# Low halves of streamed weights: from a VectorE subtraction to a ScalarE negation and an accumulating DMA

## Chip, cores and metric

The kernel runs on one core of a Trainium2 chip. The metric is the device time of one execution in microseconds (us). An execution is also recorded by the hardware profiler; its trace gives the start and duration of every instruction and DMA packet. Engines are named as in the profile: PE is TensorE, with PEld for its weight loads, DVE is VectorE, ACT is ScalarE, POOL is GpSimd, SP is SyncE. SP does no arithmetic here; it issues DMAs.

## The reference, cut to what matters

A two-layer trunk on 16 meta tokens and 512 frames of width 1024, in float32. Layer 0 mixes by two kinds of attention, layer 1 by retention in chunks; each layer ends with a squared-ReLU MLP of width 4096, and a layer norm stands behind each half.

```python
for layer in range(DEPTH):                       # DEPTH = 2
    i = layer // 2
    if layer % 2 == 0:
        mix = _even_mixer(h, even_w_in[i], ..., even_w_out[i], layer)
    else:
        mix = _retention(h, ret_w_in[i], ret_w_out[i])
    h = _layer_norm(DEEPNORM_ALPHA * h + mix, ln_g[layer, 0], ln_b[layer, 0])
    h = _layer_norm(DEEPNORM_ALPHA * h + _sq_relu_mlp(h, ffn_w1[layer], ffn_w2[layer]),
                    ln_g[layer, 1], ln_b[layer, 1])
```

All matrices together are 224 tiles of 128 x 1024 floats (512 KB), each used once.

## The kernel before

**Two halves.** A float32 product is made of three passes of a faster format, fp32r. Every operand is split into a high half, the value rounded to fp32r, and a low half, the value minus the high half. A product is high x high + high x low + low x high (`PASSES`, issued in `product`), so for each block of a weight the third matmul is the first that reads the weight's low half. On the chip's page the halves of weights are `wh` and `wl`.

**How a weight comes.** `weight_plan` lists the tiles in the order of use. `prepare` (line 211) takes the next: it takes one of three raw buffers (`rpool`), has SP load the tile from HBM into it (line 223), and calls `halves` (line 226). There ScalarE casts the raw tile to `wh` (line 228), and VectorE subtracts, `wl` = raw - `wh` (line 229). The raw buffer is free for a later load when both have read it. `weights` (line 264) is called by each product for its tile, and first prepares tiles until two ahead of it exist. The halves live in `upool`, 43 buffers that all other large tiles share.

**Quads.** For three quarters of each MLP's first matrix the kernel computes a 2 x 2 block product from seven block products instead of eight. `quad_steps` (line 232) prepares such a quad from two raw tiles, r0 and r1, in five steps: the halves of r0 ("11" and "22"), sums of blocks of r0 and r1 (lines 242, 248, 250) with their own halves ("a" to "d"), and the halves of one half of r1, named `w12` in the code (lines 252 and 253). `quad_up` (line 1138) multiplies; its results go through the banks qa to qd, and ScalarE and VectorE turn them into `tv`, `up` and `g`. There are 24 quads.

**Other stages.** A stage that ends in a layer norm is written by `tail`, which runs its last six tiles over the first half of the positions and then over the second, so that the norm of one half runs beside products of the other. `begin` starts the next MLP with the first half that is ready.

**What sets the order.** A scheduler orders each engine's instructions when the program is built; an engine then runs its own list strictly in order and waits at semaphores. A wait of ScalarE for a product, say, also holds a cast that stands behind it. SP's list holds DMAs alone. GpSimd has no work but four small memsets at the start.

The subtraction that the diff replaces is line 229 when it is called for a raw tile, and line 253. The halves of sums (line 229 on `sums`) stay as they are, and so do the first four tiles, which are loaded by `load` (line 369) instead of SP's plain call.

Of the kernel before, what the change touches and what calls it, by code (L numbers as in the profile page):

```python
# [9 lines left out]
F32R = mybir.dt.float32r  # L10
AF = mybir.ActivationFunctionType
ALU = mybir.AluOpType
# [100 lines left out]
def plan_tiles(plan):  # L113
    first, n = [], 0
    for item in plan:
        first.append(n)
        n += 2 if item[0] == "Q" else 1
    return first
# [3 lines left out]
def kernel(  # L122
# [19 lines left out]
    nc = tc.nc  # L142
    act, dve = nc.scalar, nc.vector
# [18 lines left out]
    first_tile = plan_tiles(plan)  # L162
# [8 lines left out]
    def both(dt=F32, name="u"):  # L171
        return upool.tile([P, 2, L], dt, tag="u", name=name)
# [5 lines left out]
    def flat(dt, name):  # L178
        return both(dt, name).rearrange("p a b -> p (a b)")[:, :1024]

    def raw_tile():
        return rpool.tile([P, 1024], F32, tag="raw", name="raw")
# [10 lines left out]
    def f(t):  # L193
        return t.bitcast(F32)

    def dup(t, n):
        return t.rearrange("p (o n) -> p o n", o=1).broadcast_to([P, 2, n])
# [8 lines left out]
    queue = {"next": 0, "used": 0, "ready": []}  # L206
# [4 lines left out]
    def prepare(load=nc.sync.dma_start):  # L211
        i = queue["next"]
        if i == len(plan):
            return
        queue["next"] += 1
        if plan[i][0] == "Q":
            quad = {}
            quad["steps"] = quad_steps(quad, first_tile[i])
            next(quad["steps"])
            queue["ready"].append(quad)  # L220
            return
        raw = raw_tile()
        load(out=raw, in_=w[first_tile[i]])
        queue["ready"].append(halves(raw))

    def halves(raw):
        wh, wl = flat(F32R, "wh"), flat(F32R, "wl")
        act.copy(out=wh, in_=raw)  # L228
        dve.tensor_tensor(out=wl, in0=raw, in1=f(wh), op=ALU.subtract)  # L229
        return wh, wl  # L230

    def quad_steps(quad, at):
        lo, hi = slice(0, 512), slice(512, 1024)
        r0, r1 = raw_tile(), raw_tile()
        nc.sync.dma_start(out=r0, in_=w[at])
        nc.sync.dma_start(out=r1, in_=w[at + 1])
        yield
        h, l = halves(r0)
        quad["11"], quad["22"] = (h[:, lo], l[:, lo]), (h[:, hi], l[:, hi])
        yield  # L240
        s0 = flat(F32, "sums")
        dve.tensor_tensor(out=s0.rearrange("p (a b) -> p a b", a=2), in0=r0.rearrange("p (a b) -> p a b", a=2),  # L242
                          in1=dup(r1[:, hi], 512), op=ALU.add)
        yield
        h, l = halves(s0)
        quad["c"], quad["a"] = (h[:, lo], l[:, lo]), (h[:, hi], l[:, hi])
        s1 = flat(F32, "sums")
        dve.tensor_tensor(out=s1[:, lo], in0=s0[:, hi], in1=r0[:, lo], op=ALU.add)
        yield
        dve.tensor_tensor(out=s1[:, hi], in0=s1[:, lo], in1=r1[:, lo], op=ALU.add)  # L250
        t = flat(F32R, "w12")
        act.copy(out=t[:, lo], in_=r1[:, lo])
        dve.tensor_tensor(out=t[:, hi], in0=r1[:, lo], in1=f(t)[:, lo], op=ALU.subtract)
        quad["12"] = t[:, lo], t[:, hi]
        yield
        h, l = halves(s1)
        quad["b"], quad["d"] = (h[:, lo], l[:, lo]), (h[:, hi], l[:, hi])
# [6 lines left out]
    def weights(kind, ahead=2):  # L264
        while queue["next"] < min(len(plan), queue["used"] + 1 + (1 if kind == "Q" else ahead)):
            prepare()
        assert plan[queue["used"]][0] == kind
        queue["used"] += 1
        if kind == "Q":
            quad = queue["ready"].pop(0)  # L270
            for _ in quad["steps"]:
                pass
            return quad
        wh, wl = queue["ready"].pop(0)
        k, n = {"A": (8, P), "B": (2, 512), "C": (4, 256)}[kind]
        return tuple(t.rearrange("p (k n) -> p k n", k=k, n=n) for t in (wh, wl))
# [92 lines left out]
    def load(out, in_):  # L369
        dma = nc.sync.dma_start(out=out, in_=in_)  # L370
        if loads["last"] is not None:
            after(dma, loads["last"])
        loads["last"] = dma
        return dma

    prepare(load)
    for j in range(KT // 2):
        raw = both(F32, "xf")
        for i in range(2):
            load(raw[:, i, :], x[2 * j + i])  # L380
        for i in range(2):
            pair = both(F32R, "s")
            xs.append(split(raw[:, i, :], dst=(pair[:, 0, :], pair[:, 1, :])))
            act.copy(out=hm[:, 2 * j + i, :4 * META].rearrange("p (a c n) -> p a c n", a=2, c=2),
                     in_=f(pair)[:, :, :META].rearrange("p a (o n) -> p a o n", o=1).broadcast_to([P, 2, 2, META]))
        if j < 3:
            prepare(load)
# [459 lines left out]
    for h in range(8):  # L847
# [5 lines left out]
        else:  # L853
            if h == 6:
                for j in range(KT // 2):
                    t = both(F32, "y")
# [378 lines left out]
    for k, (ps, outs, pairs) in enumerate(early):  # L1235
        for i in (6, 7):
# [5 lines left out]
                lambda span, t=ht: layer_norm(span, 0, t))  # L1242
# [236 lines left out]
```

## Time and profile before

| | us |
|---|---|
| three runs: lowest, median, highest | 1528.26, 1532.27, 1533.14 |
| the profiled execution, its own time | 1526.21 |
| its span in the profile | 1524.4 |
| TensorE busy | 1485.1 |
| VectorE busy | 922.8 |
| ScalarE busy | 609.4 |

The span is the time from the first instruction to the last in the trace. The granted clock of TensorE was 0.994 on average. The page's second part cuts the span into 40 slices and shows tenths of busy time in each:

```profile
PE   8999999999999999999999999999999999999997
...
DVE  4574466677758576568534354254477848676567
ACT  4474444536324233245343442153445524233323
...
DMA  6111102141313323243014035022150313313221
```

TensorE has hardly a slice under 9, and the transfers come in bursts. In a row of groups, the text after the engine is operation, what is written <- what is read, and the shapes; then the count, the busy total, the mean of one in ns, and the idle time ahead of them with what ended it.

### The profile page before, as it was taken

The page shows a single profiled execution, that of the slowest core. Times are in us where ns is not written, and L with a number is a line of the kernel's source. Part 1 is how long each engine was busy: PE and PEld are TensorE (multiplying, and loading weights), DVE is VectorE, ACT ScalarE, POOL GpSimd, SP SyncE. Part 2 cuts the span into 40 slices and gives each one's busy share as a digit, 9 for nine tenths or more (in the row PEclk, how much of TensorE's full clock was granted, in tenths as well). Part 3 has the DMA queues.
Part 4 walks back from the last instruction along what each step waited for, and adds up shares of the span by engine and source line. Part 5 has one row for each costly group of instructions (what it writes and reads, how often), then busy time and mean ns, then how long its engine had stood idle before and what let it go on. Part 6 is the DMA issues. An engine that isn't in the chain of part 4 may idle for free.

```text
span 1524.4 us, 23188 instructions
## 1 busy us (share of the span) xinstructions
PE 1485.1 (97%) x9752; PEld 1334.4 (88%) x9752; DVE 922.8 (61%) x1522; ACT 609.4 (40%) x972; POOL 0.2 (0%) x4
## 2 busy tenths in 40 slices
PE   8999999999999999999999999999999999999997
PEld 6887878799999999999888888888899888898986
DVE  4574466677758576568534354254477848676567
ACT  4474444536324233245343442153445524233323
POOL 0000000000000000000000000000000000000000
PEclk9999999999999999999999999999999999999999
DMA  6111102141313323243014035022150313313221
GB/s 243 51 48 55 56 29 85 57 138 32 97 55 91 116 70 125 71 132 117 28 42 137 14 109 166 0 89 90 56 168 27 111 56 97 124 62 133 83 70 56
DMA packets 39593, 129.02 MB, mean 85 GB/s; under 512 B 4725, under 2 KB 7173, under 8 KB 39489
## 3 DMA queue, kind: packets, MB, share of 16 engines
q1 hardware_dynamic: 39488, 127.54, 26.1%
q8 instruction: 76, 1.25, 0.3%
q14 instruction: 29, 0.23, 0.0%
HBM read 125.43 MB, written 2.10 MB: 84 GB/s over the span
## 4 chain that ended last, share of the span: by engine, by line
PE 86%; DVE 9%; ACT 2%; DMA 2%; issue 1%; ACTq 0%; DVEq 0%
PE bank L156 33%; PE mm L156 21%; PE v_ps L156 10%; PE qc L156 5%; PE o_ps L156 5%; PE s_ps L156 4%; DVE wl L229 3%; PE qa L156 3%; DMA raw<-in_w 2%; PE qd L156 2%; ACT wh L228 1%; PE t_ps L159 1%; PE qb L156 1%; PE sum_ps L156 1%; DVE up L1182 1%
## 5 line engine op out<-in xcount | busy, mean ns | idle before, releaser
L229 DVE TENSOR_TENSOR wl<-raw,wh 128x1024 fp32r<-128x1024 f32 x200 | 242.3, 1221 | 71.6 <-ACT wh L228 70.9
L228 ACT CAST wh<-raw 128x1024 fp32r<-128x1024 f32 x200 | 205.9, 1046 | 107.7 <-DMA raw<-in_w 75.8
L156 PE MATMUL bank<-g,wh 128*128 128x512 f32 (+2 forms) x800 | 202.3, 344 | 3.4 <-ACT g L1183 2.9
L156 PEld LDWEIGHTS bank<-g,wh 128*128 128x128 f32 x800 | 138.4, 190 | 22.0 <-ACT g L1183 3.1
L156 PE MATMUL bank<-hh,wh 128*128 128x512 f32 (+3 forms) x448 | 144.2, 337 | 0.0
L156 PE MATMUL bank<-hh,wl 128*128 128x512 f32 (+3 forms) x448 | 140.4, 330 | 0.0
L156 PE MATMUL mm<-g,wh 128*128 128x264 f32 x832 | 136.5, 286 | 2.5 <-ACT g L1183 2.0
L156 PE MATMUL bank<-g,wl 128*128 128x512 f32 (+2 forms) x400 | 136.5, 342 | 0.0
L156 PE MATMUL bank<-hl,wh 128*128 128x512 f32 (+3 forms) x448 | 120.8, 331 | 4.3 <-DVE hl L948 4.3
L156 PEld LDWEIGHTS mm<-g,wh 128*128 128x128 f32 x832 | 116.3, 190 | 2.9 <-ACT g L1183 2.2
L156 PE MATMUL qc<-tc,wh 128*128 128x264 f32 (+1 forms) x576 | 107.1, 284 | 2.0 <-ACT wh L228 1.8
L156 PEld LDWEIGHTS bank<-hh,wh 128*128 128x128 f32 x448 | 84.0, 188 | 10.7 <-ACT hh L960 1.2
L156 PE MATMUL mm<-s,wh 128*128 128x264 f32 x544 | 92.8, 292 | 0.5 <-DVE s L362 0.5
L156 PEld LDWEIGHTS qc<-tc,wh 128*128 128x128 f32 x576 | 89.0, 188 | 3.6 <-ACT wh L228 3.3
L156 PEld LDWEIGHTS bank<-hh,wl 128*128 128x128 f32 x448 | 83.9, 188 | 8.4
L156 PE MATMUL qc<-tc,wl 128*128 128x264 f32 (+1 forms) x288 | 82.5, 287 | 5.3 <-DVE wl L229 5.1
L156 PE MATMUL mm<-g,wl 128*128 128x264 f32 x416 | 85.0, 286 | 0.0
L156 PEld LDWEIGHTS bank<-hl,wh 128*128 128x128 f32 x448 | 72.6, 188 | 14.0 <-DVE hl L948 4.9
L156 PEld LDWEIGHTS bank<-g,wl 128*128 128x128 f32 x400 | 75.5, 189 | 9.3
L228 ACT CAST wh<-sums 128x1024 fp32r<-128x1024 f32 x48 | 50.4, 1049 | 76.8 <-DVE sums L242 32.5
L156 PEld LDWEIGHTS mm<-s,wh 128*128 128x128 f32 x544 | 74.9, 188 | 6.8 <-issue 2.3
L229 DVE TENSOR_TENSOR wl<-sums,wh 128x1024 fp32r<-128x1024 f32 x48 | 58.6, 1221 | 27.6 <-PE mm L156 10.3
(314 smaller groups left out, 3098.5 us busy)
## 6 DMA issues: line engine op xcount, KB each, us to landing
raw<-in_w SPq DMA_DIRECT2D x224, 512.0 KB, 4.1
xf<-in_x SPq DMA_DIRECT2D x8, 264.0 KB, 5.4
y<-in_x SPq DMA_DIRECT2D x8, 264.0 KB, 4.1
out<-y SPq DMA_DIRECT2D x8, 256.0 KB, 2.2
nb<-in_c_nb SPq DMA_DIRECT2D x4, 264.0 KB
rd<-in_c_rd SPq DMA_DIRECT2D x4, 256.0 KB
rd<-in_c_rm SPq DMA_DIRECT2D x4, 192.0 KB, 4.2
fm<-in_c_fm SPq DMA_DIRECT2D x1, 264.0 KB, 2.7
```

The lines of the kernel that those rows point to most:

```text
L156: return self.put(nc.tensor.matmul(*a, **k))
L159: return self.put(nc.tensor.transpose(*a, **k))
L228: act.copy(out=wh, in_=raw)
L229: dve.tensor_tensor(out=wl, in0=raw, in1=f(wh), op=ALU.subtract)
L1182: dve.scalar_tensor_tensor(out=rs, in0=rs, scalar=0.0, in1=rs, op0=ALU.max, op1=ALU.mult)
```

## The change

For each raw tile that SP loads, ScalarE makes both halves' first steps, and a DMA issued by GpSimd does the arithmetic. ScalarE casts raw to `wh` as before, and then writes -`wh` into `wl`. GpSimd's DMA reads the same tile of the weights from HBM once more and adds it to what stands in `wl`. VectorE no longer reads the raw tile, except for the sums of a quad.

```diff
-        queue["ready"].append(halves(raw))
+        queue["ready"].append(rounded(raw, w[first_tile[i]]) if load == nc.sync.dma_start else halves(raw))
...
+    def rounded(raw, source, into=None):
+        wh, wl = into or (flat(F32R, "wh"), flat(F32R, "wl"))
+        act.copy(out=wh, in_=raw)
+        act.activation(out=wl, in_=f(wh), func=AF.Copy, scale=-1.0)
+        nc.gpsimd.dma_start(out=wl, in_=source, accum_op=ALU.add)
+        return wh, wl
...
-        h, l = halves(r0)
+        h, l = rounded(r0, w[at])
...
         t = flat(F32R, "w12")
-        act.copy(out=t[:, lo], in_=r1[:, lo])
-        dve.tensor_tensor(out=t[:, hi], in0=r1[:, lo], in1=f(t)[:, lo], op=ALU.subtract)
+        rounded(r1[:, lo], w[at + 1][:, lo], (t[:, lo], t[:, hi]))
```

The lines below 224 keep their numbers; those behind `halves` stand 6 or 7 further down.

The built programs show where the scheduler puts these steps. ScalarE, in the first MLP behind the last quad of a group: g (L1183, after the change L1189) is the cast of a quad's result, and the six casts that follow it are of the next tiles of the second matrix. Before:

```order
L1183 CAST g<-up 128x1056
L228 CAST wh<-raw 128x1024 x6
L228 CAST wh<-sums 128x1024
L252 CAST w_5922<-raw 128x512
L228 CAST wh<-sums 128x1024
L228 CAST wh<-raw 128x1024
L1165 COPY tv<-qa 128x264
```

After, the same place; the number behind `w` is a buffer's:

```order
L235 ACTIVATE wl<-wh 128x1024
L228 CAST wh<-sums 128x1024
L234 CAST w_5985<-raw 128x512
L235 ACTIVATE w_5985<-w_5985 128x512
L228 CAST wh<-sums 128x1024
L234 CAST wh<-raw 128x1024
L235 ACTIVATE wl<-wh 128x1024
L1171 COPY tv<-qa 128x264
```

Each cast of a raw tile (L234 now) has its negation (L235) directly behind it, so that the sixth cast stands behind five negations, and the copy `tv` behind one.

VectorE, inside a quad of the first MLP; `sums` are the sums of blocks and their halves are L229 on `sums`. Before:

```order
L229 TENSOR_TENSOR wl<-raw,wh 128x1024
L242 TENSOR_TENSOR sums<-raw 128x1024
L1167 TENSOR_TENSOR tv<-qb,tv 128x264
L1180 TENSOR_TENSOR up<-qc,tv 128x264
L1169 TENSOR_TENSOR tv<-qc,tv 128x264
L1182 SCALAR_TENSOR_TENSOR up<-up 128x1056
L229 TENSOR_TENSOR wl<-sums,wh 128x1024
L248 TENSOR_TENSOR sums<-sums,raw 128x512
L253 TENSOR_TENSOR w_5159<-raw,w_5159 128x512
L1184 TENSOR_TENSOR g<-up,g 128x1056
L250 TENSOR_TENSOR sums<-sums,raw 128x512
L229 TENSOR_TENSOR wl<-sums,wh 128x1024
```

After, the same quad:

```order
L249 TENSOR_TENSOR sums<-raw 128x1024
L1173 TENSOR_TENSOR tv<-qb,tv 128x264
L1175 TENSOR_TENSOR tv<-qc,tv 128x264
L229 TENSOR_TENSOR wl<-sums,wh 128x1024
L255 TENSOR_TENSOR sums<-sums,raw 128x512
L1186 TENSOR_TENSOR up<-qc,tv 128x264
L257 TENSOR_TENSOR sums<-sums,raw 128x512
L1188 SCALAR_TENSOR_TENSOR up<-up 128x1056
L1190 TENSOR_TENSOR g<-up,g 128x1056
L229 TENSOR_TENSOR wl<-sums,wh 128x1024
```

The two subtractions on raw tiles are gone, and the second sum (L250, now L257) stands ahead of the two steps on `up` and `g` instead of behind them.

## The prediction

> **What bounds the kernel now.** I read the page's first part, then the waits of TensorE, then the groups of the lines that the diff touches. The page, engine by engine and then its chain of work:
>
> ```profile
> span 1524.4 us, 23188 instructions
> ...
> PE 1485.1 (97%) x9752; PEld 1334.4 (88%) x9752; DVE 922.8 (61%) x1522; ACT 609.4 (40%) x972; POOL 0.2 (0%) x4
> ...
> PE 86%; DVE 9%; ACT 2%; DMA 2%; issue 1%; ACTq 0%; DVEq 0%
> ```
>
> TensorE is busy 97% of the span. VectorE and ScalarE have room, so taking work from VectorE pays only where TensorE waits for VectorE. The view of waits, for the matmul engine (total us, times, longest):
>
> ```profile
> PE qc L156 <- DVE wl L229: 5.1, 7, 1.0
> PE bank L156 <- DVE hl L948: 4.3, 3, 1.4
> ...
> PE qc L156 <- ACT wh L228: 1.8, 4, 0.7
> ```
>
> These three are the waits in which the changed VectorE work can have a part: 5.1 + 1.8 in the quads, 4.3 in the layer norms, **11.2 us together**. That is all a lighter VectorE can bring, under 1%. Everything else is risk.
>
> **What is removed and added.** The groups, with count, busy total and mean ns of one:
>
> ```profile
> L229 DVE TENSOR_TENSOR wl<-raw,wh 128x1024 fp32r<-128x1024 f32 x200 | 242.3, 1221 | 71.6 <-ACT wh L228 70.9
> L253 DVE TENSOR_TENSOR w<-raw,w 128x512 fp32r<-128x512 f32 x24 | 16.4, 682 | 0.0
> L228 ACT CAST wh<-raw 128x1024 fp32r<-128x1024 f32 x200 | 205.9, 1046 | 107.7 <-DMA raw<-in_w 75.8 <-PE bank L156 21.0 <-PE mm L156 9.4
> L252 ACT CAST w<-raw 128x512 fp32r<-128x512 f32 x24 | 14.8, 617 | 28.8 <-PE mm L156 15.1 <-PE bank L156 13.7
> ```
>
> Four of the 200 subtractions stay (the tiles loaded at the start). VectorE loses 196 x 1.221 + 24 x 0.682 = 256 us and falls to about 667 us (44%). ScalarE gains a second pass of the same shape behind each cast: 196 x 1.05 + 24 x 0.62 = 221 us, to 830 us (54%). Neither becomes the bound. GpSimd, which had no DMA, issues 220: 196 of 512 KB and 24 of 256 KB, 109 MB read from HBM once more. What the 16 DMA engines do now, and how long a weight load takes from issue to landing:
>
> ```profile
> q1 hardware_dynamic: 39488, 127.54, 26.1%
> ...
> raw<-in_w SPq DMA_DIRECT2D x224, 512.0 KB, 4.1
> DMA to landing us min/median/max: 3.3/4.1/6.6
> ```
>
> 127.54 MB took 26.1% of 1524 us, 398 us of all engines, so 512 KB (0.524 MB) take 1.64 us of them.
>
> **What lies on the path.** Before, a low half was ready a cast and a subtraction after its raw tile. Now it is ready a cast, a negation (1.05 us) and the landing of an accumulating DMA later; call that landing X. What decides is how long before its first use each low half is cast. I took the end of the cast and the first matmul that reads the `wl`, for all 196 tiles. The spare between the two falls into classes, shown here by one place of each, and for the third by its first, a typical and its last place (each pair: ScalarE's cast, TensorE's first use; columns start, duration):
>
> ```profile
> 665.96 2.94 ACT L228 CAST wh<-raw 128x1024 fp32r<-128x1024 f32 x3
> 670.62 0.41 PE L156 MATMUL mm<-g,wl 128*128 128x264 f32 x2
> ...
> 819.92 1.04 ACT L228 CAST wh<-raw 128x1024 fp32r<-128x1024 f32 x1
> 826.91 0.39 PE L156 MATMUL v_ps<-wl,hh 128*128 128x512 f32 x1
> ...
> 298.18 2.94 ACT L228 CAST wh<-raw 128x1024 fp32r<-128x1024 f32 x3
> 307.34 0.29 PE L156 MATMUL bank<-s,wl 128*128 128x264 f32 x1
> ...
> 1294.32 2.00 ACT L228 CAST wh<-raw 128x1024 fp32r<-128x1024 f32 x2
> 1302.80 0.39 PE L156 MATMUL bank<-g,wl 128*128 128x512 f32 x1
> ...
> 1470.85 1.05 ACT L228 CAST wh<-raw 128x1024 fp32r<-128x1024 f32 x1 [3.24 <-DMA raw<-in_w]
> 1479.98 0.28 PE L156 MATMUL bank<-g,wl 128*128 128x256 f32 x1
> ```
>
> - Class A, 2 places (666 and 1465): the cast ends at 667.0, the use is at 670.6, spare 3.6 us.
> - Class B, 2 places (820 and 1036): 826.9 - 821.0 = 5.9 us.
> - Class C, 34 places from 298 to 1471: 8.1, 7.4 and 8.1 us in the three pairs shown (the first cast of a merged row ends 1.05 us after its start), 7.3 to 8.2 in all.
> - All other tiles have 9 us or more, most over 12.
>
> A low half is late by 1.05 + X - spare. The matmul that waits for it holds everything behind it on TensorE, whose queue is in order, and the evacuations behind that. On GpSimd only later accumulates stand behind one that waits for its negation. Lateness adds up over places, because most of these casts stand in ScalarE's order behind the evacuation of a product: TensorE late means cast late. Tiles that are cast before the stall ahead of them is over share it, and I counted them once.
>
> X is shown by no row. From below it is bounded by the plain load's 4.1 us: same bytes, same source, same 16 engines. The pieces that I can price on top are the second stream, since the old contents of `wl` must be read as well, 1.64 us, and a collision with a raw load, another 1.64: the cast that frees a raw buffer lets SP issue the next load (its queue waits for that buffer now), and the accumulate starts a negation later, in the middle of it. That is **X = 4.1 + 1.64 + 1.64 = 7.3 us**, the value I take. From above I use 10 us, twice a load's 4.1 plus one stream.
>
> At X = 7.3 a tile needs 8.35 us after its cast. Class A loses 2 x 4.75 = 9.5, class B 2 x 2.4 = 4.8, class C 34 places with 0.5 on average (the last partly covered by the stall ahead) = 17.7: **32 us**. At X = 4.1 only class A is left, 2 x 1.6 = 3 us. At X = 10 the same count gives 127 us, since class C then loses over 30 us for each us of X and tiles with 9 us of spare join. The answer is flat up to X = 6.5 and steep behind it.
>
> **The gain.** In a quad the rows that matter are VectorE's, and ScalarE's cast that waits for them:
>
> ```profile
> 460.74 1.22 DVE L229 TENSOR_TENSOR wl<-raw,wh 128x1024 fp32r<-128x1024 f32 x1
> ...
> 466.94 0.68 DVE L253 TENSOR_TENSOR w<-raw,w 128x512 fp32r<-128x512 f32 x1
> ...
> 469.48 1.05 ACT L228 CAST wh<-sums 128x1024 fp32r<-128x1024 f32 x1 [3.03 <-DVE sums L250]
> ...
> 331.59 1.22 DVE L229 TENSOR_TENSOR wl<-raw,wh 128x1024 fp32r<-128x1024 f32 x1
> ...
> 334.02 1.22 DVE L229 TENSOR_TENSOR wl<-raw,wh 128x1024 fp32r<-128x1024 f32 x1
> ```
>
> The subtractions at 460.74 and 466.94 go, 1.9 us of a run of VectorE without a gap, and the new order puts the last sum ahead of the `g` work too. The waits there are 1.0 us at the longest, so I credit 6.9 us in full. The two subtractions at 331.59 and 334.02 stand ahead of the first half's norm (`rs`, then `hh`, `hl`); 2.4 us against waits of 1.4 us: 4.3 us in full. The low half of w12 has a cast of 0.62 behind it and 10 us to its use; it costs nothing below X = 9.
>
> **Bursts.** Where a stage takes weights faster, transfers may queue. Two such stretches (last columns: DMA's share, GB/s):
>
> ```profile
> 665.00:690.00 25.00, 23.46 (x178) 23.24 (x179) 15.82 (x16) 12.59 (x13) 0.00 (x0) 0.93 0.62 202
> ...
> 1110.00:1135.00 25.00, 24.89 (x191) 23.76 (x189) 18.09 (x24) 9.46 (x9) 0.00 (x0) 1.00 0.79 240
> ```
>
> The first uses 0.62 x 25 = 15.5 us of the engines. Its 12 tiles would add 12 x 1.64 = 20 us at one stream: 35 us of transfers in 25. Half of those tiles are used 30 us later, so between 0 and 10 us are lost; I take 4 us in each of three such stretches (665, 1110, 1465), 12 us.
>
> The Trainium skill, "DMA: Bandwidth & Descriptors", section "Issuing engines are not separate DMA queues", has it that GpSimd's transfers run on the same sixteen engines as SP's and interleave with them; no run here shows a second queue. If that failed, the collision and the bursts would drop out, and the sum would be 1526 - 11 + 8 = 1523 us (X = 5.7).
>
> **The sum.** The profiled execution took 1526.2 us (span 1524.4 and 1.8 around it): 1526.2 - 11.2 + 32 + 12 = **1559 us**. The three other runs have a median of 1532.3, 6 us more, so for a median of runs I add 6: 1565 us.
>
> **Rivals.**
>
> 1. *The accumulate lands like a load* (X 4 to 5.5 us). For it: the same bytes, a landing of 3.3 us at best, and 74% of the engines' time free. Against it: two streams instead of one, and a start right behind a load. Stalls of 3 to 7 us against 11.2 of gain, no bursts: 1518 to 1522, with the 6 us 1524 to 1528. This is the side on which the change wins; it decides itself at X = 6.3, where stalls and gain are equal. The Trainium skill's page "DMA: Bandwidth & Descriptors", section "Anatomy of one DMA — SWDGE (gpsimd) path", fits a GpSimd DMA by 2.0 us + bytes/436e3; that makes 3.2 us for 512 KB, an estimate, 4.4 us with the bytes counted twice, and the sum would be 1519 by it. The load's row of 4.1 us is longer than the fit, and the fit is not of an accumulating transfer.
> 2. *The adding itself is slow* (X of 10 us and over, or the queue backs up behind itself). For it: nothing here shows the rate of an adding transfer, and an accumulate comes every 6.9 us on average (1524 / 220), so a service time near that leaves no room. 1526.2 - 11.2 + 127 + 30 = 1672 at X = 10, and 40 us more for each further us.
> 3. *ScalarE's order delays the evacuations.* The negation of a quad's `r0` stands ahead of the copy `tv`, so 24 quads x 1.05 = 25 us if TensorE had to wait for that copy, with a quick accumulate: 1526 - 4 + 25 = 1547, with the 6 us 1553. Against it: TensorE's waits list no copy of ScalarE there.
>
> **How the numbers follow.** Forecast (X 6 to 9 us) 0.45, rival 1 0.28, rival 2 0.22, rival 3 0.05. The likeliest gives 1565. The range takes in the bounds of X, from 1520 to 1670; beyond it stay about half of rival 2 and a little of rival 1. The forecast's own range is 1535 to 1615. A difference of 0.3% (4.6 us) is about what can be told from no change: rival 1 ends under 1527.7 in 0.21 and within the bound in 0.07, the forecast's lower end falls within it in 0.06, and the rest is slower: faster 0.21, same 0.13, slower 0.66.
>
> **What would show it.** The group of VectorE's L229 from `raw` shrinks to 4 and a ScalarE group `wl<-wh` of 196 at 1.05 us appears. The list of DMA issues gets `wl<-in_w`, and its landing is X: under 6 us rival 1, over 9 rival 2. TensorE's waits must name that DMA, first for `mm<-g` near 670 with some 5 us, then for many places of under 1 us. The waits for `wl` L229 in `qc` and for `hl` L948 should be gone; if they stay, the gain was mis-assigned. I would be wrong if X is short, or if casts come earlier because SP gets its raw buffers back a subtraction sooner.

## The result and the profile after

| | before | after |
|---|---|---|
| median of the runs, us | 1532.7 (4 runs, 1528.3 to 1536.5) | 1576.6 (4 runs, 1574.5 to 1578.2) |
| ratio, 95% interval | | 1.0287 [1.0256, 1.0318] |
| the profiled execution, own time | 1526.2 | 1578.2 |
| span | 1524.4 | 1576.5 |
| TensorE busy | 1485.1 | 1500.1 |
| TensorE idle between its first and last matmul | 22.1 | 58.8 |

The change makes the kernel 2.9% slower. The forecast was 1565 us, 11.6 us too low. The page of the profile after, the lines that answer to those shown of before:

```profile
PE 1500.1 (95%) x9752; PEld 1342.4 (85%) x9752; DVE 687.3 (44%) x1302; ACT 822.7 (52%) x1192; POOL 190.7 (12%) x224
DMA  8543424593747678589058289176494757969661
...
q0 software_dynamic: 31680, 109.07, 38.2%
q1 hardware_dynamic: 39488, 127.54, 23.8%
...
L236 POOL DMA_DIRECT2D wl<-in_w x196 | 169.8, 866 | 1180.8 <-ACT wl L235 900.2
...
raw<-in_w SPq DMA_DIRECT2D x224, 512.0 KB, 5.4
wl<-in_w POOLq DMA_DIRECT2D x196, 512.0 KB, 9.0
```

VectorE fell to 44% as worked out and ScalarE rose to 52%; neither bounds anything. The new thing is the queue q0: it moves 109 MB and takes 38.2% of 1576.5 us of the engines, 602 us, which is 2.9 us for each 512 KB. A plain load on q1 still takes 1.5 us for the same bytes. The accumulate lands 9.0 us behind its issue in the median, and a load 5.4 us behind it, where it was 4.1 before. TensorE's waits after the change (us in total, times, longest):

```profile
PE bank L156 <- DMA wl<-in_w: 17.4, 13, 4.2
PE mm L156 <- DMA wl<-in_w: 12.0, 6, 4.2
PE v_ps L156 <- DMA wl<-in_w: 6.8, 5, 2.1
PE bank L156 <- DVE hl L954: 4.3, 3, 1.5
```

TensorE now waits 24 times for an accumulate, 36.2 us. The waits of `qc` for `wl` and `wh` are gone, and the wait for `hl` in the layer norms stands where it stood: 4.3 us, three times. The same view for the weight loader (PEld), of before and then of after, gives larger sums for the same waits:

```profile
PEld qc L156 <- DVE wl L229: 7.2, 9, 1.2
...
PEld qc L156 <- ACT wh L228: 3.3, 6, 0.9
```

```profile
PEld bank L156 <- DMA wl<-in_w: 23.3, 18, 4.5
PEld mm L156 <- DMA wl<-in_w: 13.3, 6, 4.4
PEld v_ps L156 <- DMA wl<-in_w: 8.7, 5, 2.4
```

10.5 us in `qc` before, where the matmul engine's rows had 6.9, and 45.3 us for the accumulates after, where they had 36.2. The records of matmuls overlap: those of 256 columns are drawn 0.28 us long and start 0.12 us apart, so the last one ahead of a wait covers some 0.16 us of it, and that part counts as busy time. Which of the two sums is the real one can be read from the six stretches of quads, from the first to the last matmul into `qa` to `qd`: they took 284.6 us before and 274.1 after, 10.5 less. There it is the weight loader's. For the accumulates I take the weight loader's sum as well; no stretch shows it by itself.

The third part is TensorE's clock. The windows of the profile after around 1509 us (length, TensorE busy, granted clock):

```profile
1502.50:1509.30 6.80, 4.12 (x24) 1.00 0.00 0
1509.30:1522.90 13.60, 8.75 (x20) 0.50 0.83 200
1522.90:1529.70 6.80, 6.80 (x45) 1.00 1.06 246
```

The granted clock is 1.00 or 0.50, and it is at half for multiples of 3.41 us. The trace's record of it has 10.2 us at half before the last matmul in the profile of before, and 41.0 us after the change, of which TensorE was idle for 7.9. At half clock, half of the busy time is lost: 5.1 us before, (41.0 - 7.9) / 2 = 16.5 us after.

So the 52.1 us between the two spans come from: the accumulates' waits +45.3, the quads -10.5, the half clock +11.4, and other idle time of TensorE, short waits at the start and in the norms, +7.4 (58.8 - 22.1 = 36.7, less 36.2 for the accumulates, plus 6.9 that the quads lost). That makes 53.6, 1.5 more than the spans differ.

### The profile page after: what moved, and what is told of

Its sections match the earlier page's. It is cut to its first block, busy times and chain, and to the rows that moved or that the text cites. A ratio compares the mean times of both kernels' runs of the same rounds, so it can differ in the third digit from the quotient of the medians.

```text
span 1576.5 us, 23765 instructions
## 1 busy us (share of the span) xinstructions
PE 1500.1 (95%) x9752; PEld 1342.4 (85%) x9752; DVE 687.3 (44%) x1302; ACT 822.7 (52%) x1192; POOL 190.7 (12%) x224
## 3 DMA queue, kind: packets, MB, share of 16 engines
q0 software_dynamic: 31680, 109.07, 38.2%
## 4 chain that ended last, share of the span: by engine, by line
PE 45%; issue 15%; DMA 9%; DVE 2%; ACT 2%; POOL 1%; POOLq 0%; ACTq 0%; DVEq 0%
PE bank L156 19%; PE mm L156 8%; PE qc L156 5%; DMA raw<-in_w 5%; DMA wl<-in_w 4%; PE qa L156 4%; PE v_ps L156 3%; PE qb L156 2%; PE qd L156 2%; POOL wl L236 1%; ACT wh L234 1%; PE s_ps L156 1%; PE o_ps L156 1%; PE sum_ps L156 0%; ACT wl L235 0%
## 5 line engine op out<-in xcount | busy, mean ns | idle before, releaser
L236 POOL DMA_DIRECT2D wl<-in_w x196 | 169.8, 866 | 1180.8 <-ACT wl L235 900.2
L234 ACT CAST wh<-raw 128x1024 fp32r<-128x1024 f32 x196 | 204.2, 1042 | 103.5 <-DMA raw<-in_w 81.7
L235 ACT ACTIVATE wl<-wh 128x1024 fp32r<-128x1024 f32 x196 | 207.6, 1059 | 5.5
L156 PEld LDWEIGHTS mm<-g,wh 128*128 128x128 f32 x832 | 119.6, 195 | 3.3 <-ACT g L1189 2.2
L156 PEld LDWEIGHTS bank<-hh,wl 128*128 128x128 f32 x448 | 85.2, 191 | 11.2 <-DMA wl<-in_w 2.8
L156 PEld LDWEIGHTS bank<-g,wl 128*128 128x128 f32 x400 | 75.7, 190 | 20.5 <-DMA wl<-in_w 11.4
L1100 DVE TENSOR_TENSOR y<-y,bank 128x256 f32<-128x256 f32 (+2 forms) x56 | 28.8, 516 | 120.7 <-PE bank L156 120.5
```

The costliest lines, as they stand in the source:

```text
L156: return self.put(nc.tensor.matmul(*a, **k))
L235: act.activation(out=wl, in_=f(wh), func=AF.Copy, scale=-1.0)
L236: nc.gpsimd.dma_start(out=wl, in_=source, accum_op=ALU.add)
L1100: dve.tensor_tensor(out=on(y, span), in0=on(y, span), in1=ps, op=ALU.add)
```

## The experiments

The theory after the result: an accumulate costs time where its landing is longer than the spare of its tile, and stalls of TensorE bring half-clock stretches on top; VectorE's lighter work is worth something in the quads alone. Rivals: ScalarE's second pass delays others; GpSimd's queue or the doubled bytes are what is slow; all accumulates together load the engines too much.

**The change without its DMA** (the negation stays, VectorE subtracts behind it):

```diff
-        nc.gpsimd.dma_start(out=wl, in_=source, accum_op=ALU.add)
+        dve.tensor_tensor(out=wl, in0=raw, in1=f(wh), op=ALU.subtract)
```

> The change without its DMA: ScalarE casts and negates as after the change, and VectorE then writes raw - wh into wl as before. Theory (the loss is the landing of the accumulate against the spare, and half clock behind the stalls): without the DMA no low half is late, TensorE's idle time falls from 59 us back to about 22 us, the half-clock time from 41 us to about 10 us, and the time is 1528 to 1540 us, within 0.5% of before. Rival, ScalarE's second pass delays the evacuations: the time stays above 1550 us, with TensorE waiting for ScalarE's tv copy or for a cast, and the gaps stand where they stand after the change.

Measured: 1535.4 us against 1530.9, ratio 1.0021 [0.9999, 1.0043]; idle 23.5 us, half clock 37.5 us. The DMA is the loss: without it 1.0021 is left of 1.0287. The half-clock time did not fall, and that is a miss: it is no fixed price of the accumulates. And the near-zero is a sum of two things. The quads took 274.4 us, 10 less than before, although VectorE still makes every subtraction. Outside the quads this profile is 21 us longer than that of before. Some 13 us of them are half clock, (37.5 - 1.9) / 2 against 5.1 us; the other 8 are idle time of TensorE. For that I see a wait that the change does not have, and no run tests it: VectorE's subtraction stands at the head of its queue until the negation is there. VectorE's group:

```profile
L236 DVE TENSOR_TENSOR wl<-raw,wh 128x1024 fp32r<-128x1024 f32 x196 | 239.6, 1224 | 124.1 <-ACT wl L235 123.4
```

Negations ended 123.4 us of its idle time; before, casts ended 70.9. And the largest sum of TensorE's waits in this kernel is for a norm's sums, which VectorE makes; it was 1.1 us before:

```profile
PE sum_ps L156 <- DVE acc L919: 6.4, 2, 3.8
```

**The change with a plain DMA** in place of the accumulating one; it leaves out the addition, so the low half holds the raw weights:

```diff
-        nc.gpsimd.dma_start(out=wl, in_=source, accum_op=ALU.add)
+        nc.gpsimd.dma_start(out=wl, in_=source)
```

> The change with a plain DMA in place of the accumulating one: same bytes, same queue, same order, nothing is added, so that the low half holds the raw weights and the output is another one. Theory (the adding itself costs the engines, 2.9 us per 512 KB against 1.5 for a load): the landing of wl falls from 9.0 to 5 to 6 us, its share of the engines' time from 38% to about 21%, TensorE's waits for that DMA from 36 us to about 8 us (the places with 3.6 us of spare), and the time is about 1540 us. Rival, the software queue or the doubled bytes are what is slow: landing stays over 8 us and the time over 1565 us.

Measured: 1542.9 us, ratio 1.0087 [1.0062, 1.0112]. The queue on the page and GpSimd's group:

```profile
q0 software_dynamic: 31680, 109.07, 22.7%
...
L236 POOL DMA_DIRECT2D wl<-in_w x196 | 103.6, 529 | 1213.2 <-ACT wl L235 900.1
```

The landing of `wl` here, and then in the change itself:

```profile
DMA to landing us min/median/max: 3.7/6.1/9.7
```


```profile
DMA to landing us min/median/max: 5.2/9.0/14.6
```

The same packets take 22.7% of 1539.4 us, 1.7 us for 512 KB in place of 2.9, and land in 6.1 us in place of 9.0. GpSimd needs 0.53 us to issue one, an accumulate 0.87. The weight loader's waits for `wl` are 14.8 us in place of 45.3, 30.5 less; the two ratios differ by 0.020 of 1531 us, 31 us. So of the waits the adding has about two thirds, and the rest comes with any transfer there.

**The same transfers, needed later.** `product` makes all passes with the high half of a weight first, those with its low half last:

```diff
-        for k in range(lo, hi):
+        for k, i in [(k, i) for k in range(lo, hi) for i in (0, 1)] + [(k, 2) for k in range(lo, hi)]:
```

> The change with the passes of a product in another order: all blocks of a tile first make the passes with the high half of the weight, then all make the pass with its low half; so the low half is first needed 3 to 4 us later, and nothing else is changed. Theory (latency against spare): places with a spare of 7.3 to 8.2 us get 11 or more, those with 3.6 get about 7; of 36 us of waits for the DMA 10 to 15 us stay, half-clock time falls to about 20 us, and the time is 1540 to 1555 us. Rival, contention of the transfers or ScalarE's load sets the time: it stays within 5 us of the change's 1577 us, as the transfers and ScalarE's work are the same.

Measured: 1563.0 us, ratio 1.0214 [1.0182, 1.0247]. The direction is the theory's: the same 109 MB and the same ScalarE, 14 us less than the change (11 by the two ratios), and the matmul engine's waits for `wl` fell from 36.2 to 15.4 us. The size is not: I had 1540 to 1555. Half-clock time stayed at 44.4 us, and there was a new wait of 5.0 us of `mm` for `o`, which the control below does not have; why it comes was not followed up. The control has the order of passes without any accumulate:

> The control of low_last: the kernel before with the same order of passes (all passes with the high halves first, the pass with the low halves last). Theory (the order by itself costs nothing, and low_last's 32 us over before are its 15 us of waits for the accumulate and half clock): 1526 to 1535 us. Rival (the order delays the last sums and evacuations: low_last showed new waits of mm for o, 5.0 us, and of sum_ps for sq, 4.5 us): 1538 to 1550 us, with these waits present without any accumulate.

Measured: 1529.4 us, ratio 0.9974 [0.9955, 0.9993]. The order by itself costs nothing.

**The quads left out, and the quads alone.** In the first, `quad_steps` calls `halves` again for r0 and subtracts on VectorE for w12; in the second, `prepare` does:

```diff
-        h, l = rounded(r0, w[at])
+        h, l = halves(r0)
```

```diff
-        queue["ready"].append(rounded(raw, w[first_tile[i]]) if load == nc.sync.dma_start else halves(raw))
+        queue["ready"].append(halves(raw))
```

> The change only in prepare (148 tiles); in the quads r0 and w12 go back to VectorE's subtraction. Theory (the quads lose nothing and gain 7 us, the loss is in the dense products): 1577 to 1585 us, the waits of qc for VectorE's wl (5 us) and for ScalarE's wh (2 us) come back, and TensorE's waits for the accumulate stay at 30 us or more. Rival, the quads' own accumulates crowd the engines and lengthen landing elsewhere: the time falls to 1560 us or less.

> The change only in the quads (24 tiles r0 and 24 halves w12); prepare's tiles keep VectorE's subtraction. Theory (VectorE's lighter work in the quads is worth the 7 us of waits that are gone after the change, and the accumulates there come in time): 1523 to 1530 us against a before of 1531, ratio 0.994 to 0.999, no wait of qc for wl or wh, and under 3 us of waits for the accumulate. Rival (r0's low half, with 7.3 to 8 us of spare in six quads, is late, or the waits of qc turn up in another bank): ratio 1.000 to 1.008.

Measured: 1581.5 us without the quads, ratio 1.0333 [1.0297, 1.0368], waits of `qc` for VectorE and ScalarE back with 4.8 us. The quads alone: 1514.8 us, ratio 0.9898 [0.9874, 0.9921], **faster than before**, by more than I expected. No wait of `qc` is left, none for an accumulate, and the six stretches of quads take 272.8 us, 11.8 less. The six r0 with 7.3 to 8 us of spare are not late: a negation of 1.05 us and a landing of 5.5 us fit into them. Leaving out the other accumulates is not what does it. In the change itself 18 of these 24, those issued inside the stretches of quads, land in 5.2 to 6.9 us, and no matmul of a quad waits for one there either. The landing in quads_only:

```profile
DMA to landing us min/median/max: 5.2/5.5/7.9
```

**Tiles by their spare.** 83 of the 172 tiles of `prepare` had less than 15 us between the cast and the first use of the low half in the profile of before. One kernel leaves these 83 to VectorE and keeps all other accumulates (89 tiles and the quads); the other gives the accumulate to these 83 alone.

```diff
-        ... rounded(raw, w[first_tile[i]]) if load == nc.sync.dma_start else halves(raw))
+        ... rounded(raw, w[first_tile[i]]) if load == nc.sync.dma_start and i not in SHORT else halves(raw))
```

> The change, except for the 83 of prepare's 172 tiles that had less than 15 us between their cast and the first use of their low half before the change; those keep VectorE's subtraction. 89 tiles of prepare, and r0 and w12 of all 24 quads, keep the accumulating DMA. Theory (a tile costs time only where its spare is short): TensorE's waits for the accumulate fall from 36 us to under 5, its waits of qc stay gone (7 us), and the time is 1523 to 1533 us, 0 to 0.5% under before. Rival (the load on the engines or the DMAs that all accumulates make together): half of the accumulates are left, so about half of the loss, 1550 us or more.

> The other way round: only those 83 tiles take the accumulating DMA, the 89 with more spare and the quads keep VectorE's subtraction. Theory (spare): TensorE's waits for the accumulate stay at 25 to 36 us, and the time is 1565 to 1580 us. Rival (load of all accumulates together): 83 of 220 accumulates, about 1550 us, with waits under 18 us since the landing is shorter.

Measured: 1520.0 us with the long ones, ratio 0.9927 [0.9909, 0.9945], and 1585.1 us with the short ones, ratio 1.0355 [1.0332, 1.0378]. Both sizes lie outside what I expected, the first 3 us below its range and the second 5 us above. The direction settles it: 83 accumulates make the whole loss, and more of it than all 220, because the quads' gain is missing. The 89 others with the quads lose nothing, although they land just as late. TensorE's only wait for an accumulate with the long ones, and their landing:

```profile
PE qa L159 <- DMA wl<-in_w: 0.3, 1, 0.3
```

```profile
DMA to landing us min/median/max: 5.2/9.2/14.5
```

TensorE's waits with the short ones:

```profile
PE bank L159 <- DMA wl<-in_w: 14.6, 12, 4.3
PE mm L159 <- DMA wl<-in_w: 8.6, 6, 4.4
...
PE v_ps L159 <- DMA wl<-in_w: 5.9, 4, 3.3
```

29.1 us of waits against 36.2 in the change, from well under half of its transfers. TensorE was idle 39.8 us longer than before here; beside the accumulates, the waits for a norm's sums (`acc`) rose to 7.8 us. The rival of a common load has 1550 us in both expectations and is out.

**What the quads gain by.** neg_only kept every subtraction and had the quads' gain. What it shares with the change is an order: the subtraction of r0, which waits for the negation, stands behind the first sum on VectorE instead of ahead of it. So the kernel before with this one move:

```diff
-        h, l = halves(r0)
+        h, l = flat(F32R, "wh"), flat(F32R, "wl")
+        act.copy(out=h, in_=r0)
...
                           in1=dup(r1[:, hi], 512), op=ALU.add)
+        dve.tensor_tensor(out=l, in0=r0, in1=f(h), op=ALU.subtract)
```

> The kernel before with one move and no new instruction: in a quad VectorE makes the first sum (s0) ahead of the subtraction of r0, as it does after the change and in neg_only, where the negation holds the subtraction back. No negation, no accumulating DMA. Theory (the quads gain by the order of VectorE, not by its lighter load; neg_only kept every subtraction, and its quads still took 10 us less than before): the quads take 272 to 276 us against 284.6 before, the waits of qc for wl and wh are gone, and the time is 1514 to 1523 us. Rival (the gain of quads_only needs the subtraction off VectorE): 1527 us or more and waits of qc of 4 us or more.

Measured: 1519.9 us, ratio 0.9934 [0.9909, 0.9959]. VectorE in the same quad (start, duration), before, where the subtraction shown at 460.74 stands between these two, and then in this kernel:

```profile
460.40 0.42 DVE L1176 TENSOR_TENSOR up<-qc,tv 128x264 f32<-128x264 f32 x1
...
461.87 1.22 DVE L242 TENSOR_TENSOR sums<-raw 128x1024 f32<-128x1024 f32 x1
```

```profile
465.44 0.42 DVE L1178 TENSOR_TENSOR up<-qc,tv 128x264 f32<-128x264 f32 x1
465.78 1.22 DVE L243 TENSOR_TENSOR sums<-raw 128x1024 f32<-128x1024 f32 x1
466.92 1.22 DVE L245 TENSOR_TENSOR wl<-raw,wh 128x1024 fp32r<-128x1024 f32 x1
```

The first sum (465.78) now starts ahead of the subtraction (466.92), 0.34 us behind the start of `up` instead of 1.47, so 1.1 us earlier. The cast and the low half that `qc` waited for hang on it, and no wait of `qc` is left. The windows of the six stretches of quads, first row and sum, of before and then of this kernel:

```profile
438.10:498.70 60.60, 58.22 (x472) 1.00 0.33 96
...
sum 284.60, PE 277.24; mean PE 46.21
```

```profile
443.70:501.20 57.50, 57.50 (x472) 1.00 0.32 101
...
sum 274.40, PE 274.39; mean PE 45.73
```

10.2 of the 11.8 us of quads_only come without a negation, without a DMA, and with VectorE's load unchanged. The two ratios' intervals overlap, and of the 5 us between the medians the clock has most: the runs of quads_only have a median granted clock of 0.993 and those of sum_first 0.9905, which is about 4 us of 1520.

**Both gains together:** sum_first, and the quads alone, each with the order of passes of low_last.

> sum_first with the order of passes of before_low_last. Theory (both gains are separate: the quads' 12 us and the order's 4 us): 1510 to 1518 us. Rival (the order's 4 us were a difference of half-clock stretches): equal to sum_first within 2 us.

> quads_only (the accumulating DMA for r0 and w12 alone) with the order of passes of before_low_last. Theory (as for sum_low): 1508 to 1515 us, 2 to 5 us under quads_only's 1515. Rival: equal to quads_only within 2 us. Against sum_low it tells what VectorE's lighter load in the quads is worth beside the order: nothing if the two are within 2 us.

Measured: 1517.9 us, ratio 0.9921 [0.9895, 0.9946], and 1520.1 us, ratio 0.9936 [0.9916, 0.9957]. The order of passes adds nothing that can be told: 2 us less in one pair, 5 us more in the other, where I had expected 2 to 5 us less in the second. Its 0.26% in the control alone is no gain that I would count on.

**The kernel before, profiled once more:**

> The kernel before once more, for a second profile of it. Theory (the half-clock stretches differ from one execution to the next, as a stretch of idle TensorE is followed by one or not): the same waits and about 22 us of idle TensorE, but another number of half-clock stretches, and TensorE busy 1485 to 1493 us. Rival (the half clock belongs to the kernel): the same three stretches of 3.4 us, 1485 us busy, within 1 us.

Measured: 1523.5 us in one run, TensorE idle 21.1 us, busy 1483.5. Again three stretches of 3.41 us at half clock, so the number that I expected to differ did not. But they are not the same three. The windows (length, busy, granted clock) of the first profile of before, then of the second:

```profile
117.60:120.90 3.30, 3.30 (x9) 0.50 0.51 158
...
1151.00:1155.00 4.00, 2.63 (x16) 1.00 0.02 4
```

```profile
116.00:119.50 3.50, 3.50 (x16) 1.00 0.52 171
1149.10:1152.30 3.20, 3.11 (x12) 0.50 0.00 0
```

Both have an idle stretch of 1.54 us near 115 and one of 1.4 us, at 1151.9 in the first and 1147.8 in the second; each was followed by half clock in one execution and not in the other.

## Why the prediction was right, and where not

- **What bounds** was right: with TensorE at 97%, no work taken from VectorE could bring more than about 1%, and the best kernel here is 1.0% faster. The figure of 11.2 us was low: quads_only gains some 16 us, 11.8 of them in the quads, and its runs have a higher granted clock (median 0.993) than those of before (0.989).
- **The credit in the quads, "6.9 us in full"**, was right in its place and too small: 10.5 us. The step that failed is the view: I summed the matmul engine's waits, and a wait begins on the weight loader, 0.2 to 0.4 us earlier each time. Its cause was named among others ("the new order"), but the credit was put on the lighter load. sum_first shows that the order is nearly all of it.
- **The credit in the layer norms, "2.4 us against waits of 1.4 us: 4.3 us in full"**, failed altogether. VectorE after the change, at that place:

```profile
341.97 0.43 DVE L1102 SCALAR_TENSOR_TENSOR y<-y,bank 128x264 f32<-128x264 f32 x1 [2.50 <-PE bank L156]
342.41 0.43 DVE L903 TENSOR_SCALAR rs<-sum_ps 128x264 f32<-128x264 f32 x1
```

  Where the second subtraction stood VectorE now idles for 2.50 us until TensorE has made `bank`, and `rs`, which opens the chain to `hl`, comes no earlier. This is one of three norms; the other two I did not look at, but the sum of the three waits, 4.3 us, did not change. The subtractions had stood in a wait for TensorE. The wait could be seen before, as a short idle time behind the second subtraction:

```profile
334.02 1.22 DVE L229 TENSOR_TENSOR wl<-raw,wh 128x1024 fp32r<-128x1024 f32 x1
335.53 0.43 DVE L1096 SCALAR_TENSOR_TENSOR y<-y,bank 128x264 f32<-128x264 f32 x1 [0.28 <-PE bank L156]
```

- **The spare and X** carried the forecast. The mechanism held, and X as one number did not. Class A near 680 us (ScalarE's cast and negation, GpSimd's issue, TensorE's use):

```profile
675.52 1.04 ACT L234 CAST wh<-raw 128x1024 fp32r<-128x1024 f32 x1
676.59 1.06 ACT L235 ACTIVATE wl<-wh 128x1024 fp32r<-128x1024 f32 x1
...
677.94 0.86 POOL L236 DMA_DIRECT2D wl<-in_w  x1 [16.95 <-ACT wl L235]
...
685.39 0.81 PE L156 MATMUL mm<-g,wl 128*128 128x264 f32 x2 [4.22 <-DMA wl<-in_w]
```

  From the negation's end at 677.65 to the use at 685.39 are 7.7 us, X was 7.3; the wait is 4.2, forecast 4.75. The matmul engine's waits by class: A 8.4 (forecast 9.5), B 5.5 (4.8), the one burst with waits, 1152 to 1166 us, 4.9 (forecast three of 4), the other fourteen 17.4 (class C 17.7). Together 36.2 against 44, and 45.3 by the weight loader. That the sum came out is in part luck: class C was 34 places with 0.5 us, measured were fourteen with 1.2 on average, and two of the three bursts cost next to nothing beside class A. X is no constant. In the trace of the change it goes with the accumulates that are in flight when one is issued: 6.0 us in the median with none (65 of the 196), 7.8 with one, 11.1 with two, 12.6 with three. In the burst, GpSimd's first two issues and the first two uses:

```profile
1145.15 0.86 POOL L236 DMA_DIRECT2D wl<-in_w  x1 [7.97 <-ACT wl L235]
1147.18 0.86 POOL L236 DMA_DIRECT2D wl<-in_w  x1 [1.17 <-ACT wl L235]
...
1152.71 0.39 PE L156 MATMUL bank<-yh,wl 128*128 128x256 f32 x1 [2.23 <-DMA wl<-in_w]
...
1156.59 0.38 PE L156 MATMUL bank<-yh,wl 128*128 128x256 f32 x1 [0.26 <-DMA wl<-in_w]
```

  ScalarE lets an accumulate go every 2.0 us, and they land 3.9 us apart: each takes 2.9 us of the engines, and the raw load that comes with it 1.5, together more than 2.0. The longest landings fell on tiles with long spares, as by_spare shows: 14.5 us at the longest and 0.3 us of waits. The pieces of X were put together wrongly, too: a second stream of 1.64 us was close, as an accumulate took 2.9 us of the engines and a plain transfer 1.7, but even a plain transfer of this queue landed 2 us later than a load of before (6.1 against 4.1), and later than SP's loads beside it (4.5).
- **Rival 1, lands like a load**, is out for the change as a whole (9.0 us), and true for the tiles of the quads (5.5 us), where the change wins. The Trainium skill, "DMA: Bandwidth & Descriptors", section "Anatomy of one DMA — SWDGE (gpsimd) path", would give 3.2 us for 512 KB, an estimate; the quickest plain transfer took 3.7 and the median 6.1, so in traffic the trace disagrees.
- **Rival 2, the adding itself is slow**, was half right: the adding is two thirds of the waits, by 1.2 us more of the engines' time for a tile and 3 us more of landing, but X stayed under 10 in the median. That the queue backs up behind itself came true in bursts, up to 14.6 us, and not on average, since an accumulate comes every 7 us.
- **Rival 3, ScalarE delays evacuations**, is out: no wait for `tv`, and 89 tiles with negations are free.
- **Not foreseen: the clock**, 11.4 us between the profiles, and 7.4 us of other idle time. With them the sum is 1526.2 - 10.5 + 45.3 + 11.4 + 7.4 = 1579.8 against the measured 1578.2. The 6 us that I added for the median belong to this as well: the profile of before was an execution with little half clock (granted clock 0.994, where the 43 runs of it beside the experiments have a median of 0.989), that of after was 1.6 us above its median.

## What to carry to other kernels

Before a step is replaced by one with a longer latency, list for each instance the time between its input and its first use; the sum of what falls short is the price, with the latency that the step has among its own kind in a burst; moving only the instances with spare can turn a loss into nothing. Where an engine's work is removed ahead of a wait, look whether that engine is idle between the removed step and the awaited one: if it is, nothing will move. And before load is taken off an engine at all, try its order: one sum ahead of one subtraction brought 0.7% here.

## What was not expected of the hardware

Behind the first mixer the half clock follows short idle stretches, by chance. In the 14 profiles of this study, all 52 stretches at half clock behind 330 us have at least 1.0 us of idle TensorE in the 3.41 us ahead of them. Of the idle stretches of 2.5 us and more, 30 of 35 were followed by one within 3.5 us; of 1.6 to 2.5 us, 9 of 25; of 1.2 to 1.6 us, 14 of 59; of 0.6 to 1.2 us, 1 of 71. The 24 stretches ahead of 330 us, in the first mixer, have no such idle time ahead in 21 cases, and why they come stays open. The times of two executions of one kernel can so differ with no difference in the program. Of the 43 runs of the kernel before, the 11 with a granted clock of 0.992 or more have a mean span of 1524.3 us, and the 15 with 0.988 or less 1531.7. The profiles:

| kernel | ratio | span | idle | at half clock |
|---|---|---|---|---|
| before, two profiles | | 1524.4, 1521.7 | 22.1, 21.1 | 10.2, 10.2 |
| after | 1.0287 | 1576.5 | 58.8 | 41.0 |
| neg_only | 1.0021 | 1534.9 | 23.5 | 37.5 |
| plain_dma | 1.0087 | 1539.4 | 32.0 | 30.7 |
| short_only | 1.0355 | 1585.2 | 61.9 | 47.8 |
| by_spare | 0.9927 | 1516.7 | 14.8 | 20.5 |
| quads_only | 0.9898 | 1508.5 | 15.2 | 3.4 |
| sum_first | 0.9934 | 1521.1 | 16.2 | 27.3 |

quads_only and sum_first differ by 1 us of idle time and by 12 us in these spans, and 24 us more at half clock are those 12 us. No run put an idle stretch in by itself, so that the idle time causes the half clock is read from these counts, not shown by an experiment. The Trainium skill, "TensorE: Matmul & The Clock Gate", section "Part 1: The HAM clock gate", has the clock halved after at least one idle window of about 3.4 us that runs free of the program. The 3.41 us and the chance agree; the length does not, since half clock followed gaps of 1.2 to 1.6 us 14 times in 59.

An accumulating DMA from HBM costs more than its bytes: 2.9 us of the engines for 512 KB against 1.7 for the plain one of the same queue, 0.87 against 0.53 us of GpSimd for the issue, and 9.0 against 6.1 us to land.
